# Queries and keys of one attention layer: computed with the channels on the partitions instead of the tokens

## The chip, the core and the metric

The kernel runs on one core of one Trainium2 chip. The metric is the device time of one execution in microseconds, as a median over runs. TensorE (PE) multiplies into PSUM banks of 512 f32 columns; VectorE (DVE), ScalarE (ACT) and GpSimd (POOL) work beside it, each through its own list of instructions in a fixed order; SyncE (SP) issues most of the DMAs, also in order.

## The reference

One layer: attention beside a state-space branch on the same normalised input, then an expert feed-forward part. The change touches only how `q` and `k` are made:

```python
q, k, v, z, xbc, dt_raw, gates = jnp.split(h @ w_in, IN_SPLITS, axis=-1)      # h: 1024 latent tokens x 1024
q = apply_rope(q.reshape(nb, ns, 8, 2, 64), cos, sin)
k = apply_rope(k.reshape(nb, ns, 8, 2, 64), cos, sin)
kc = (hc @ w_k).reshape(nb, nl, 8, 2, 64)                                     # hc: 256 context tokens, not rotated
k_all = jnp.concatenate([kc, k], axis=1)

def apply_rope(u, cos, sin):
    rot = jnp.concatenate([-u[..., 32:], u[..., :32]], axis=-1)
    return u * cos + rot * sin
```

A head has two components of 64 channels. The rotation mixes channel i of a component with channel i + 32, by the cosine and sine of the token's place.

## The kernel before

**Precision.** Every f32 operand is split into a high part (`hi`, `hh`) and a low rest (`lo`, `hl`), and each product is three matmuls (`mm3`, L419): high by high and two mixed ones.

**The stage.** `norm_and_qkv` (L491) normalises the ten token tiles of 128 (two of context, eight of latents), transposes them on PE (`modulate`, tiles `tr`), scales them (`hf`) and splits them into `hh` and `hl`, with the model channel on the partitions. The tokens are three groups g: 0 is the context (256 tokens), 1 and 2 are 512 latent tokens each. While the first inputs arrive, PE also makes the modulation vector (`ada`: tiles `wa`, `adab`). A second set of modulation products, `ada_late`, runs on DVE during the stage (tiles `wada`, `wacc`: eight instructions for each 512 KB loaded).

**The blocks.** `main` goes through six blocks of 512 output columns: k0, v0, q0, k1, v1, q1. Before the change each block goes token tile by token tile: for a tile, 24 matmuls with `hh` or `hl` (128 x 128, tokens) as the loaded operand and 512 weight columns streamed give tokens x 512 channels in one of four PSUM banks `acc`. In the first block the first three tiles are done by halves of the model channels, so that PE can begin with half of the weights.

**After a tile of q or k** comes `post_qk` (L661). A latent tile goes through three products on DVE (`ra`, and `rb` in two halves, with the table `rope`), a sum on POOL (`r`), four transposes on PE (f32, 128 x 128) into a bank `tr`, a copy by ACT to `sa` (the high part), a subtraction on DVE to `sb` (the low part), and, for every second tile, four or eight stores of `sa` and `sb` to the scratch tensor `qk` in DRAM. A context tile has a plain copy in the place of products and sum. `v` tiles are copied by ACT and stored.

**The order.** The kernel is written as generators; a scheduler (`Flow`, with estimated durations) interleaves them when the kernel is built, so what is written elsewhere may shift the order of instructions on every engine. The chip then follows that order. The mixer (`mixer_t`) begins when block q1 and all its `post_qk` are issued; its first piece is `dt` (16 + 16 matmuls of 512 columns and 16 of 256 with `hi`, folded by ten small matmuls `aux<-fold,G`, then a chain of DVE and ACT to the tile `dtn`), beside the first product of its convolution (`acc<-hh,hi` and so on).

Of the kernel before, what the change touches and what calls it, by code (L numbers as in the profile page):

```python
# [9 lines left out]
F32 = mybir.dt.float32  # L10
F32R = mybir.dt.float32r
# [3 lines left out]
ALU = mybir.AluOpType  # L15
# [4 lines left out]
P = 128  # L20
D = 1024
KC = 8
T = 1024
# [352 lines left out]
class Layer:  # L376
# [114 lines left out]
    def norm_and_qkv(s):  # L491


        nc, tc, I, F = s.nc, s.tc, s.I, s.F
# [7 lines left out]
        spans = [(0, 2), (2, 4), (6, 4)]  # L502
# [7 lines left out]
        acc = s.ring(pp, [P, 512], "acc", 4)  # L510
# [9 lines left out]
        st = {"wa": [], "x": 0, "w": 0, "normed": 0, "mod": 0, "done": [set(), set(), set()], "cols": 0, "blocks": 0, "ada": False, "q": None, "two": {}}  # L520
# [106 lines left out]
        def parts(g, k, hf, w):  # L627
# [5 lines left out]
            hfs.put(hf)  # L633
            st["done"][g].add(k)

        def weights():
            for n, (kind, j) in enumerate(blocks):
                c0 = {"q": COL_Q, "k": COL_K, "v": COL_V}[kind] + j * 512
                for a in (0, 4):
                    yield [raws, lambda: st["x"] >= (10 if n else AW0[a // 4]), "NOW"]  # L640
                    raw = raws.get()
                    F.dma(raw, win[:, a:a + 4, c0:c0 + 512])
                    st["w"] += 1
                    yield [lambda: sets[n % 2] is not None]
# [3 lines left out]
                    yield from s.splits([(hi[:, b:b + 2], lo[:, b:b + 2], raw[:, b:b + 2]) for b in (0, 2)],  # L648
                                        lambda raw=raw, w=(hi, lo): (raws.put(raw), ready.append(w)), 1)

        def post_v(ps, j, tok):
# [6 lines left out]
            F.dma(s.vv[j][tok], v[:, :512].rearrange("p (h d) -> p h d", d=P))  # L658
            sas.put(v)

        def post_qk(ps, kind, j, t):  # L661
            yield [lambda: st["q"] is not None]
            rr, ras, rbs, sas, sbs, rope = (st["q"][n] for n in ("r", "ra", "rb", "sa", "sb", "rope"))
            if t < 2:
                yield [ps, rr, "ACT"]
                r = rr.get()
                F.acopy(r, ps.rearrange("p (h x) -> p h x", x=64))
                acc.put(ps)
            else:
                yield [ps, rope, ras, rbs, "DVE"]  # L670
                cs = rope[:, t - 2, :]
                pv = ps.rearrange("p (h x) -> p h x", x=64)
                ra, rb = ras.get(), rbs.get()
# [3 lines left out]
                acc.put(ps)  # L677
                yield [ra, rb, rr, "POOL"]
                r = rr.get()
                F.ptt(r, ra, rb, ALU.add)  # L680
                ras.put(ra)
                rbs.put(rb)
            yield [r, tr]
            pt = tr.get()
            for m in range(4):
                F.tp(pt[:, m * P:(m + 1) * P], r[:, 2 * m:2 * m + 2].rearrange("p u x -> p (u x)"), s.ident)
            two = st["two"].setdefault((kind, j, t // 2), [])
            yield [pt, "ACT"] + ([] if two else [sas, sbs])
            if not two:
                two += [sas.get(), sbs.get(), 0]  # L690
            a, b = two[:2]
            (av, bv), pv = (w.rearrange("p (m h c) -> h p m c", m=4, h=2)[t % 2] for w in (a, b)), pt.rearrange("p (m c) -> p m c", m=4)
            F.acopy(av, pv)
            yield [a, "DVE"]
            F.tt(bv, pv, av.bitcast(F32), ALU.subtract)
            tr.put(pt)
            two[2] += 1
            if two[2] == 2:
                o0 = (t // 2 - (kind == "q")) * 2 * P
                dst = s.qk[j].rearrange("(m u) (v x) c -> v u x m c", u=2, v=2)  # L700
                for w, v, o in ((a, 0, 0), (a, 1, 0), (b, 0, T), (b, 1, T)) if kind == "q" else ((a, 0, 2 * T), (b, 1, 2 * T)):
                    for u in range(2):
                        F.dma(dst[v, u][:, :, o + o0:o + o0 + 2 * P], w[64 * u:64 * u + 64].bitcast(F32).rearrange("x (m c) -> x m c", m=4))
                sas.put(a)
                sbs.put(b)
            rr.put(r)

        def main():
            for n, (kind, j) in enumerate(blocks):
                tiles = list(range(2 if kind == "q" else 0, 10))  # L710
                steps = [(t, 0, KC) for t in tiles]
                if n == 0:
                    steps = [(t, a, a + 4) for a in (0, 4) for t in tiles[:NH]] + steps[NH:]
                banks = {}
                for t, k0, k1 in steps:
                    yield [lambda: len(ready) >= 2 * n + k1 // 4]
                    tok = slice(t * P, (t + 1) * P)
                    g = 0 if t < 2 else 1 if t < 6 else 2
                    sl = slice((t - spans[g][0]) * P, (t - spans[g][0] + 1) * P)
                    hh, hl = s.h[g]  # L720
                    yield [lambda: st["done"][g].issuperset(range(k0, k1))] + ([] if k0 else [acc])
                    ps = banks.pop(t) if k0 else acc.get()
                    for k in range(k0, k1):
                        wh, wl = ready[2 * n + k // 4]
                        if k % 4 == 0:
                            yield [wh, wl, hh, hl]
                        s.mm3(ps, hh[:, k, sl], hl[:, k, sl], wh[:, k % 4], wl[:, k % 4], k == 0, k == KC - 1)
                    if k1 < KC:
                        banks[t] = ps
                    else:  # L730
                        F.spawn(1, post_v(ps, j, tok) if kind == "v" else post_qk(ps, kind, j, t))
# [14 lines left out]
        F.run(lambda: st["ada"])  # L746
        s.close("wa")
        qp = s.open("qkv", side="right")
        st["q"] = q = {"r": s.ring(qp, [P, 8, 64], "r", 2), "ra": s.ring(qp, [P, 8, 64], "ra", 2),
                       "rb": s.ring(qp, [P, 8, 64], "rb", 2), "sa": s.ring(qp, [P, 1024], "sa", 2, F32R),  # L750
                       "sb": s.ring(qp, [P, 1024], "sb", 2, F32R), "rope": qp.tile([P, 8, P], F32, name="rope")}
        F.dma(q["rope"], I["rope"].rearrange("(t p) c -> p t c", p=P))
        F.run(lambda: len(st["done"][2]) == KC)
        s.close("xp")
        qw = s.open("qkvw1", side="right")
# [1728 lines left out]
```

## Time and profile before

| what | us |
|---|---|
| median of three runs (2785.47 to 2786.71) | 2785.7 |
| the profiled execution | 2800.41 |
| its span | 2798.6 |
| stage of the six blocks, first to last matmul | 31.5 to 386.9 |
| PE busy over the span | 94% |
| mean granted TensorE clock, share of full | 0.976 |

The profiled execution is 0.5% longer than the median. PE times overlap: a matmul of 512 columns is listed with about 0.39 us from start to modelled end, while the next starts about 0.23 us after it; what a matmul costs is read from start to start. The granted clock is 1.00 at 2.4 GHz and 0.5 at 1.2 GHz; a stretch between them has part of each.

### The profile page before, as it was taken

Reading aid. Unit: us, or ns where it says so; the run is one execution under the profiler, and the core shown is the slowest. Engines: PE = TensorE matmul, PEld = TensorE weight load, DVE = VectorE, ACT = ScalarE, POOL = GpSimd, SP = SyncE. Lnnn points to the kernel's source line nnn. Section 1 sums busy time; section 2 is a strip of 40 time slices with the busy share of each in tenths; the row PEclk is TensorE's granted clock in tenths of the full one; section 3 lists DMA queues with packets and bytes.
Section 4 is the critical chain, followed back from the end, with each engine's and each line's share of the span. In section 5 each row is a group of like instructions: output and inputs, shape, how many; then the busy total and the mean of one; then the engine's idle time right before and its main releaser. Section 6 shows DMA issues by size and latency. Waiting matters only on the chain.

```text
span 2798.6 us, 41131 instructions
## 1 busy us (share of the span) xinstructions
PE 2618.5 (94%) x14561; PEld 2101.1 (75%) x14561; DVE 2013.0 (72%) x4680; ACT 1340.7 (48%) x2104; POOL 903.0 (32%) x669
## 2 busy tenths in 40 slices
PE   7999999999999999999999999889999999999991
PEld 4888878778788777888887687668887776777660
DVE  6877133768686749888894767867788877788863
ACT  4211123344443546666664422435666656676651
POOL 0111010545353520000000000055656656677841
PEclk9999999999999999999999999999999999999996
DMA  7767253242334354223233953568899998999997
GB/s 277 224 206 216 64 143 105 67 139 91 121 91 132 106 172 145 82 91 141 93 102 125 292 179 133 188 216 264 276 309 297 315 299 278 307 321 328 314 316 233
DMA packets 275409, 545.67 MB, mean 195 GB/s; under 512 B 31562, under 2 KB 166835, under 8 KB 248194
## 3 DMA queue, kind: packets, MB, share of 16 engines
q1 hardware_dynamic: 239330, 437.14, 45.6%
q0 software_dynamic: 35872, 105.88, 14.8%
q8 instruction: 115, 1.88, 0.3%
q14 instruction: 92, 0.75, 0.1%
HBM read 433.78 MB, written 124.73 MB: 200 GB/s over the span
## 4 chain that ended last, share of the span: by engine, by line
PE 58%; DMA 10%; DVE 9%; issue 4%; ACT 2%; POOL 2%; SPq 0%; POOLq 0%; ACTq 0%; DVEq 0%
PE gu L148 16%; PE acc L148 10%; PE dn L148 9%; PE bacc L148 5%; PE sps L148 5%; PE pv L148 4%; DMA cr<-cumd,crow 3%; PE xt L152 2%; PE tr L152 2%; PE aux L148 2%; DVE G L187 2%; DMA qk<-qk 2%; DMA braw<-in_w_branch_attn_dram 1%; DVE gl L171 1%; DVE W L180 1%
## 5 line engine op out<-in xcount | busy, mean ns | idle before, releaser
L171 DVE TENSOR_TENSOR gl<-raw,gh 128x1024 fp32r<-128x1024 f32 x240 | 288.2, 1218 | 35.4 <-ACT gh L164 33.7
L148 PE MATMUL acc<-hh,hi 128*128 128x512 f32 (+2 forms) x760 | 304.7, 401 | 1.3 <-DVE ux L187 1.3
L148 PE MATMUL acc<-hl,hi 128*128 128x512 f32 (+2 forms) x760 | 289.3, 381 | 0.0
L164 ACT CAST gh<-raw 128x1024 fp32r<-128x1024 f32 x240 | 246.6, 1050 | 88.0 <-PE gu L148 59.2
L148 PE MATMUL acc<-hh,lo 128*128 128x512 f32 (+1 forms) x736 | 280.9, 382 | 2.5 <-DVE lo L171 2.5
L148 PE MATMUL gu<-gh,xh 128*128 128x512 f32 (+3 forms) x672 | 278.4, 414 | 0.6 <-ACT gh L164 0.6
L148 PE MATMUL gu<-gl,xh 128*128 128x512 f32 (+3 forms) x672 | 264.5, 394 | 6.2 <-DVE gl L171 4.4
L148 PE MATMUL gu<-gh,xl 128*128 128x512 f32 (+3 forms) x672 | 264.5, 394 | 0.0
L193 DVE TENSOR_SCALAR_CACHE_REDUCE e<-sps 128x512 f32<-128x512 f32 (+1 forms) x384 | 214.4, 597 | 32.9 <-PE sps L148 32.6
L262 POOL DMA_INDIRECT cr<-cumd,crow x98 | 123.4, 1260 | 316.1 <-DMA wtab<-sc 281.2
L268 POOL DMA_INDIRECT yacc<-y,tk x98 | 181.3, 1850 | 96.8 <-issue 23.2
L148 PE MATMUL sps<-qk 128*128 128x512 f32 (+1 forms) x768 | 195.6, 386 | 9.3 <-DMA qk<-qk 5.1
L156 ACT ACTIVATE e<-e,st 128x1280 f32<-128x1280 f32 x128 | 174.7, 1366 | 32.0 <-DVE st L202 31.8
L262 POOL DMA_INDIRECT wc<-wtab,tk x98 | 148.6, 1516 | 121.0 <-DVE tk L182 85.9
L148 PE MATMUL acc<-hi,hh 128*128 128x512 f32 x448 | 181.3, 405 | 0.0
L148 PE MATMUL acc<-hi,hl 128*128 128x512 f32 x448 | 176.2, 393 | 0.4 <-DVE hl L171 0.4
L148 PE MATMUL acc<-lo,hh 128*128 128x512 f32 x448 | 176.0, 393 | 0.0
L148 PEld LDWEIGHTS sps<-qk 128*128 128x128 f32 x768 | 141.2, 192 | 41.3 <-DVE e L193 8.3
L148 PEld LDWEIGHTS acc<-hh,hi 128*128 128x128 f32 (+1 forms) x760 | 142.6, 188 | 32.9 <-issue 4.0
L148 PE MATMUL pv<-wr,vv 128*128 128x256 f32 x640 | 165.1, 381 | 0.0
L148 PEld LDWEIGHTS acc<-hl,hi 128*128 128x128 f32 (+1 forms) x760 | 142.6, 188 | 27.4 <-issue 0.8
L148 PEld LDWEIGHTS acc<-hh,lo 128*128 128x128 f32 x736 | 138.7, 188 | 32.1 <-DVE lo L171 3.3
(327 smaller groups left out, 6264.3 us busy)
## 6 DMA issues: line engine op xcount, KB each, us to landing
raw<-in_w_e_gate_dram SPq DMA_DIRECT2D x64, 1024.0 KB
raw<-in_w_e_up_dram SPq DMA_DIRECT2D x64, 1024.0 KB
draw<-in_w_e_down_dram SPq DMA_DIRECT2D x64, 1024.0 KB
qk<-qk POOLq DMA_DIRECT2D x16, 1664.0 KB
raw<-in_w_in_dram SPq DMA_DIRECT2D x40, 512.0 KB
wada<-in_w_ada_dram SPq DMA_DIRECT2D x32, 512.0 KB
R<-acd SPq DMA_DIRECT2D x64, 256.0 KB
qk<-sa SPq DMA_DIRECT2D x52, 256.0 KB
```

The costliest lines, as they stand in the source:

```text
L148: s.nc.tensor.matmul(out, l, r, start=start, stop=stop)
L152: s.nc.tensor.transpose(out, in_, ident)
L156: s.nc.scalar.activation(out, in_, fn, **kw)
L164: s.nc.scalar.copy(out, in_)
L171: s.nc.vector.tensor_tensor(out, a, b, op=op)
L180: s.nc.vector.tensor_scalar(out, a, s1, s2, op0=op0)
L187: s.nc.vector.scalar_tensor_tensor(out, a, sc, b, op0=op0, op1=op1)
L193: s.nc.vector.tensor_scalar(out, a, s1, None, op0=op0, op1=op1, accum_out=acc)
L262: s.nc.gpsimd.indirect_dma_start(out=out, out_offset=None, in_=table, in_offset=bass.IndirectOffsetOnAxis(ap=idx, axis=0), **kw)
L268: s.nc.gpsimd.indirect_dma_start(out=table, out_offset=bass.IndirectOffsetOnAxis(ap=idx, axis=0), in_=in_, in_offset=None, compute_op=ALU. ...
```

## The change

For q and k the loaded and the streamed operand change places. A unit is now (token group g, half r of the eight components, rotary half f): its 24 matmuls load 128 weight columns and stream the group's 512 (or, for the context, 256) tokens, which gives channels x tokens. To have the 32 low channels of four components in one bank and the 32 high ones in another, the weights are reordered when they are split: `byhalf` writes them as (f, k, 256 channels), reading runs of 32. Two units, f = 0 and f = 1, make a pair of banks, and `post_qk` runs once for a pair: four products on DVE (two to `sb` in f32, two to `rb`), two sums on POOL, two copies by ACT to `sa`, two subtractions on DVE in place in `sb`, then the stores (128 partitions, 512 tokens each). The context pair has two copies and two subtractions straight from its banks. There is no transpose left in it, and the rings `r`, `ra` are gone. The table `rope` becomes 128 channels x (cos, sin) x 1024 tokens. Block k0 begins with units (1,0,0), (1,0,1), (0,0,0). `v` is as before.

```diff
-    rope = np.concatenate([cos, cos, -sin, sin], axis=-1).astype(np.float32)
+    rope = np.stack([np.tile(q.T, (4, 1)) for q in (cos, sin)], axis=1).astype(np.float32)
...
+        def byhalf(w):
+            return w.rearrange("p a b -> p (a b)").rearrange("p (f k c) -> p f k c", f=2, k=4)
...
+                    if kind != "v":
+                        parts = [[byhalf(w)[:, :, b:b + 2].rearrange("p f k (y i) -> p f (k y) i", i=32) for w in (hi, lo)] +
+                                 [raw[:, b:b + 2].rearrange("p k (y f i) -> p f (k y) i", f=2, i=32)] for b in (0, 2)]
...
-                F.tt(ra, pv, cs[:, None, 0:64].to_broadcast([P, 8, 64]), ALU.mult)
-                F.tt(rb[:, :, 0:32], pv[:, :, 32:64], cs[:, None, 64:96].to_broadcast([P, 8, 32]), ALU.mult)
-                F.tt(rb[:, :, 32:64], pv[:, :, 0:32], cs[:, None, 96:128].to_broadcast([P, 8, 32]), ALU.mult)
-                acc.put(ps)
-                yield [ra, rb, rr, "POOL"]
-                r = rr.get()
-                F.ptt(r, ra, rb, ALU.add)
...
-            for m in range(4):
-                F.tp(pt[:, m * P:(m + 1) * P], r[:, 2 * m:2 * m + 2].rearrange("p u x -> p (u x)"), s.ident)
...
-            F.acopy(av, pv)
-            yield [a, "DVE"]
-            F.tt(bv, pv, av.bitcast(F32), ALU.subtract)
...
+            yield [sbs, pair[0]]
+            lo = sbs.get(F32)
+            l = [lo[:, f * 512:f * 512 + n] for f in range(2)]
+            if g:
+                cos, sin = (rope[:, i, (g - 1) * 512:g * 512] for i in range(2))
+                yield [pair[0], rope, rbs, "DVE"]
+                rb = rbs.get()
+                F.tt(l[0], pair[0], cos, ALU.mult)
+                F.tt(rb[:, 1], pair[0], sin, ALU.mult)
+                acc.put(pair[0])
+                yield [pair[1], "DVE"]
+                F.tt(rb[:, 0], pair[1], sin, ALU.mult)
+                F.tt(l[1], pair[1], cos, ALU.mult)
+                acc.put(pair[1])
+                yield [rb, "POOL"]
+                F.ptt(l[0], l[0], rb[:, 0], ALU.subtract)
+                yield [rb, "POOL"]
+                F.ptt(l[1], l[1], rb[:, 1], ALU.add)
...
+            src = l if g else [b[:, :n] for b in pair]
...
+                F.acopy(hi[:, f * 512:f * 512 + n], src[f])
...
+                F.tt(l[f], src[f], hi[:, f * 512:f * 512 + n].bitcast(F32), ALU.subtract)
...
+                    units = [(g, r, f) for g in ((0, 1, 2) if kind == "k" else (1, 2)) for r in range(2) for f in range(2)]
+                    if n == 0:
+                        units = units[4:6] + units[:4] + units[6:]
...
-                        s.mm3(ps, hh[:, k, sl], hl[:, k, sl], wh[:, k % 4], wl[:, k % 4], k == 0, k == KC - 1)
...
+                            a, b = (byhalf(w)[:, u[2], k % 4, u[1] * P:(u[1] + 1) * P] for w in (wh, wl))
+                            s.mm3(ps[:, :spans[g][1] * P], a, b, hh[:, k], hl[:, k], k == 0, k == KC - 1)
```

The order of instructions moves at three places that matter below. In the lists a name is written `out<-inputs`, for matmuls `out<-streamed,loaded`; numbers tell tiles apart (`hh_81`, `hl_82` are group 0, `hh_83`, `hl_84` group 1, `hi_172`, `lo_173` the first half of the weights of k0, `x_87` on the token tiles).

PE at the start of the stage, before: the modulation products `acc<-wa,cw`, with the first block's matmuls on the context tiles among them.

```order
L152 MATMUL tr<-cst,x_88 128x128
L148 MATMUL acc<-wa,cw 32x512 x4
L148 MATMUL acc<-hi_172,hh_81 128x512
L148 MATMUL acc<-lo_173,hh_81 128x512
L148 MATMUL acc<-hi_172,hl_82 128x512
...
L148 MATMUL acc<-wa,cw 32x512 x4
...
L148 MATMUL adab<-fold,row 128x2 x4
L152 MATMUL tr<-cst,x_89 128x128
```

PE at the same place, now:

```order
L148 MATMUL acc<-wa,cw 32x512 x8
L148 MATMUL adab<-fold,row 128x2 x4
L152 MATMUL tr<-cst,x_89 128x128
...
L148 MATMUL adab<-fold,row 128x2 x4
L152 MATMUL tr<-cst,x_87 128x128
...
L148 MATMUL acc<-hh_83,hi_172 128x512
L148 MATMUL acc<-hl_84,hi_172 128x512
L148 MATMUL acc<-hh_83,lo_173 128x512
```

The 24 matmuls on context tiles that stood among the modulation products are gone from there; the first matmul of k0 is on group 1 and stands behind all of the modulation products and behind that group's transposes.

PE at the entry of the mixer, before: the folding of `dt`, then the first convolution product, with the small products on `dtn` among its matmuls.

```order
L148 MATMUL aux<-fold,G 128x32 x10
L148 MATMUL acc<-hh_83,hi 128x512
L148 MATMUL acc<-hl_84,hi 128x512
L148 MATMUL acc<-hh_83,lo 128x512
...
L148 MATMUL aux<-dtn,cst 128x160
L148 MATMUL acc<-hh_83,hi 128x512
```

PE at the same place, now:

```order
L148 MATMUL aux<-fold,G 128x32 x10
L148 MATMUL aux<-dtn,cst 128x160 x2
L148 MATMUL aux<-dtn,cst 128x320
L148 MATMUL aux<-cst,dtn 16x128 x4
L148 MATMUL acc<-hh_83,hi 128x512
```

The products on `dtn` now stand straight behind the folding, and nine convolution matmuls that stood between are behind them. From the next products on, the order of every engine is as before.

DVE in block q0, before: products, a group of eight `wacc`, the subtraction.

```order
L171 TENSOR_TENSOR ra<-acc,rope 128x512
L171 TENSOR_TENSOR rb<-acc,rope 128x8x32 x2
L180 TENSOR_SCALAR wacc<-wada,cc 128x128
L187 SCALAR_TENSOR_TENSOR wacc<-wada,cc,wacc 128x128 x7
L171 TENSOR_TENSOR sb<-tr,sa 128x4x128
```

DVE in block q0, now:

```order
L171 TENSOR_TENSOR sb<-acc,rope 128x512
L171 TENSOR_TENSOR rb<-acc,rope 128x512 x2
L171 TENSOR_TENSOR sb<-acc,rope 128x512
L180 TENSOR_SCALAR wacc<-wada,cc 128x128
L187 SCALAR_TENSOR_TENSOR wacc<-wada,cc,wacc 128x128 x7
L171 TENSOR_TENSOR sb<-sb,sa 128x512 x2
```

A pair's four products stand together behind its second unit, and its two subtractions behind one or two groups of `wacc`.

## Rows read from the trace of the kernel before

**Rows 1.** The page: span, and the chain that ended last, by engine.

```profile
span 2798.6 us, 41131 instructions
PE 58%; DMA 10%; DVE 9%; issue 4%; ACT 2%; POOL 2%; SPq 0%; POOLq 0%; ACTq 0%; DVEq 0%
```

**Rows 2.** Windows: length, busy us (count) of PE, PEld, DVE, ACT, POOL; clock; DMA.

```profile
47.00:61.00 14.00, 13.02 (x73) 10.34 (x73) 13.13 (x49) 8.90 (x17) 0.00 (x0) 1.00 0.48 158
140.00:210.00 70.00, 69.96 (x332) 57.55 (x331) 55.67 (x132) 10.89 (x16) 8.56 (x6) 1.00 0.67 206
280.00:350.00 70.00, 68.36 (x304) 55.95 (x302) 10.69 (x16) 10.37 (x18) 1.97 (x2) 1.00 0.22 65
```

**Rows 3.** Groups of instructions by line: the removed transposes, with the idle time before them.

```profile
L152 PE MATMUL tr<-cst,r 128*128 128x128 f32 x144 | 22.1, 276 | 6.8 <-POOL r L175 6.7
```

**Rows 4.** Timeline of PE around four transposes: start, duration, instruction.

```profile
377.83 0.39 PE L148 MATMUL acc<-hi,hl 128*128 128x512 f32 x1
378.06 0.60 PE L152 MATMUL tr<-cst,r 128*128 128x128 f32 x4
...
378.73 0.39 PE L148 MATMUL acc<-lo,hh 128*128 128x512 f32 x1
```

**Rows 5.** Timeline of PE at the end of block q1.

```profile
390.00 0.66 PE L152 MATMUL tr<-cst,r 128*128 128x128 f32 x4 [2.51 <-POOL r L175]
390.42 0.47 PE L148 MATMUL acc<-hh,hi 128*64 128x512 f32 x1
```

**Rows 6.** Windows behind it, columns as in rows 2.

```profile
392.00:395.00 3.00, 3.00 (x9) 1.61 (x8) 0.01 (x1) 0.81 (x2) 0.00 (x0) 0.58 0.80 185
405.00:409.00 4.00, 3.97 (x11) 2.77 (x12) 1.65 (x4) 3.95 (x6) 0.00 (x0) 0.60 0.52 127
```

**Rows 7.** Timeline of PE and DVE at the start of the stage.

```profile
31.53 0.79 PE L148 MATMUL acc<-hi,hh 128*128 128x512 f32 x1
47.39 0.48 PE L148 MATMUL acc<-hi,hh 128*128 128x512 f32 x1
60.88 0.69 DVE L171 TENSOR_TENSOR hl<-hf,hh 128x512 fp32r<-128x512 f32 x1
61.09 0.48 PE L148 MATMUL acc<-hi,hh 128*128 128x512 f32 x1
```

**Rows 8.** Timeline of PE in the mixer: matmuls of 256 columns.

```profile
422.35 0.28 PE L148 MATMUL acc<-hh,lo 128*128 128x256 f32 x1
422.47 0.28 PE L148 MATMUL acc<-hh,hi 128*128 128x256 f32 x1
```

**Rows 9.** Groups by line: the products and the subtraction of `post_qk`.

```profile
L171 DVE TENSOR_TENSOR sb<-tr,sa 128x512 fp32r<-128x512 f32 x36 | 24.5, 685 | 11.8 <-ACT sa L164 11.8
L171 DVE TENSOR_TENSOR rb<-acc,rope 128x256 f32<-128x256 f32 x64 | 23.9, 415 | 0.0
L171 DVE TENSOR_TENSOR ra<-acc,rope 128x512 f32<-128x512 f32 x32 | 22.0, 688 | 28.1 <-PE acc L148 26.3 <-PE adab L152 1.7
```

**Rows 10.** Timeline of PE at the entry of the mixer.

```profile
401.43 2.42 PE L148 MATMUL aux<-fold,G 64*128 64x32 f32 x20
403.78 0.50 PE L148 MATMUL acc<-hh,hi 128*128 128x512 f32 x1
...
408.33 0.54 PE L148 MATMUL aux<-dtn,cst 128*128 128x160 f32 x2
```

**Rows 11.** Timeline of SP: stores of q in block q0, a store of v.

```profile
158.47 0.33 SPq L212 DMA_DIRECT2D vv<-sa  x1
199.37 3.42 SPq L212 DMA_DIRECT2D qk<-sa  x4
```

**Rows 12.** Timeline of DVE and POOL in block q0.

```profile
182.66 1.29 POOL L175 TENSOR_TENSOR r<-ra,rb 128x512 f32<-128x512 f32 x1 [3.21 <-DVE rb L171]
182.72 3.71 DVE L187 SCALAR_TENSOR_TENSOR wacc<-wada,cc,wacc 128x128 f32<-128x128 f32 x7
187.25 2.67 DVE L187 SCALAR_TENSOR_TENSOR wacc<-wada,cc,wacc 128x128 f32<-128x128 f32 x7
```

More of the change, by code (lines that the diff above doesn't have):

```diff
@@ L659, in post_v, with post_qk @@
             sas.put(v)
-        def post_qk(ps, kind, j, t):
+        def post_qk(pair, kind, j, g, r):
             yield [lambda: st["q"] is not None]
-            rr, ras, rbs, sas, sbs, rope = (st["q"][n] for n in ("r", "ra", "rb", "sa", "sb", "rope"))
-            if t < 2:
-                yield [ps, rr, "ACT"]
-                r = rr.get()
-                F.acopy(r, ps.rearrange("p (h x) -> p h x", x=64))
-                acc.put(ps)
[L669 to L673, printed above, removed]
-                F.tt(ra, pv, cs[:, None, 0:64].to_broadcast([P, 8, 64]), ALU.mult)
-                F.tt(rb[:, :, 0:32], pv[:, :, 32:64], cs[:, None, 64:96].to_broadcast([P, 8, 32]), ALU.mult)
-                F.tt(rb[:, :, 32:64], pv[:, :, 0:32], cs[:, None, 96:128].to_broadcast([P, 8, 32]), ALU.mult)
-                acc.put(ps)
-                yield [ra, rb, rr, "POOL"]
-                r = rr.get()
-                F.ptt(r, ra, rb, ALU.add)
-                ras.put(ra)
-                rbs.put(rb)
-            yield [r, tr]
-            pt = tr.get()
-            for m in range(4):
-                F.tp(pt[:, m * P:(m + 1) * P], r[:, 2 * m:2 * m + 2].rearrange("p u x -> p (u x)"), s.ident)
[L687 to L692, printed above, removed]
-            F.acopy(av, pv)
-            yield [a, "DVE"]
-            F.tt(bv, pv, av.bitcast(F32), ALU.subtract)
[L696 to L706, printed above, removed]
@@ new lines, in post_qk @@
+            rbs, sas, sbs, rope = (st["q"][n] for n in ("rb", "sa", "sb", "rope"))
+            n = spans[g][1] * P
+            yield [sbs, pair[0]]
[16 more added lines that the diff above has]
+                F.ptt(l[1], l[1], rb[:, 1], ALU.add)
+                rbs.put(rb)
@@ new lines, in post_qk @@
+            src = l if g else [b[:, :n] for b in pair]
+            yield [sas]
+            hi = sas.get()
+            for f in range(2):
+                yield [src[f], "ACT"]
+                F.acopy(hi[:, f * 512:f * 512 + n], src[f])
+            for f in range(2):
+                yield [hi, "DVE"]
+                F.tt(l[f], src[f], hi[:, f * 512:f * 512 + n].bitcast(F32), ALU.subtract)
+            if g == 0:
+                acc.put(*pair)
+            o0 = (spans[g][0] - 2 * (kind == "q")) * P
@@ L708, in main @@
+            dst = s.qk[j].rearrange("(r y) (v f i) c -> r v f y i c", y=4, v=2, f=2)
+            for f in range(2):
+                for w, v, o in ((hi, 0, 0), (hi, 1, 0), (lo, 0, T), (lo, 1, T)) if kind == "q" else ((hi, 0, 2 * T), (lo, 1, 2 * T)):
+                    F.dma(dst[r, v, f][:, :, o + o0:o + o0 + n], (w[:, f * 512:f * 512 + n].bitcast(F32) if w is hi else l[f]))
+            sas.put(hi)
+            sbs.put(lo)
         def main():
             for n, (kind, j) in enumerate(blocks):
-                tiles = list(range(2 if kind == "q" else 0, 10))
@@ L711, in main @@
-                steps = [(t, 0, KC) for t in tiles]
+                if kind == "v":
+                    units = [(0 if t < 2 else 1 if t < 6 else 2, t) for t in range(10)]
+                else:
+                    units = [(g, r, f) for g in ((0, 1, 2) if kind == "k" else (1, 2)) for r in range(2) for f in range(2)]
+                    if n == 0:
+                        units = units[4:6] + units[:4] + units[6:]
+                steps = [(u, 0, KC) for u in units]
                 if n == 0:
-                    steps = [(t, a, a + 4) for a in (0, 4) for t in tiles[:NH]] + steps[NH:]
@@ L714, in main @@
-                banks = {}
-                for t, k0, k1 in steps:
+                    steps = [(u, a, a + 4) for a in (0, 4) for u in units[:NH]] + steps[NH:]
+                banks, done = {}, {}
+                for u, k0, k1 in steps:
+                    g = u[0]
                     yield [lambda: len(ready) >= 2 * n + k1 // 4]
-                    tok = slice(t * P, (t + 1) * P)
-                    g = 0 if t < 2 else 1 if t < 6 else 2
-                    sl = slice((t - spans[g][0]) * P, (t - spans[g][0] + 1) * P)
@@ L720, in main @@
                     hh, hl = s.h[g]
                     yield [lambda: st["done"][g].issuperset(range(k0, k1))] + ([] if k0 else [acc])
-                    ps = banks.pop(t) if k0 else acc.get()
+                    ps = banks.pop(u) if k0 else acc.get()
                     for k in range(k0, k1):
@@ L726, in main @@
                             yield [wh, wl, hh, hl]
-                        s.mm3(ps, hh[:, k, sl], hl[:, k, sl], wh[:, k % 4], wl[:, k % 4], k == 0, k == KC - 1)
+                        if kind == "v":
+                            sl = slice((u[1] - spans[g][0]) * P, (u[1] - spans[g][0] + 1) * P)
+                            s.mm3(ps, hh[:, k, sl], hl[:, k, sl], wh[:, k % 4], wl[:, k % 4], k == 0, k == KC - 1)
+                        else:
+                            a, b = (byhalf(w)[:, u[2], k % 4, u[1] * P:(u[1] + 1) * P] for w in (wh, wl))
+                            s.mm3(ps[:, :spans[g][1] * P], a, b, hh[:, k], hl[:, k], k == 0, k == KC - 1)
                     if k1 < KC:
-                        banks[t] = ps
-                    else:
-                        F.spawn(1, post_v(ps, j, tok) if kind == "v" else post_qk(ps, kind, j, t))
+                        banks[u] = ps
+                    elif kind == "v":
+                        F.spawn(1, post_v(ps, j, slice(u[1] * P, (u[1] + 1) * P)))
+                    else:
+                        two = done.setdefault(u[:2], [])
+                        two.append(ps)
+                        if len(two) == 2:
+                            F.spawn(1, post_qk(two, kind, j, *u[:2]))
                 ws = ready[2 * n:2 * n + 2]
@@ L748, in norm_and_qkv @@
         qp = s.open("qkv", side="right")
[L749 to L752, printed above, removed]
+        st["q"] = q = {"rb": s.ring(qp, [P, 2, 512], "rb", 2),
+                       "sa": s.ring(qp, [P, 1024], "sa", 2, F32R),
+                       "sb": s.ring(qp, [P, 1024], "sb", 2, F32R), "rope": qp.tile([P, 2, T], F32, name="rope")}
+        F.dma(q["rope"], I["rope"])
         F.run(lambda: len(st["done"][2]) == KC)
```

5 lines of the change are left out of this document (3 added, 2 removed).

## The prediction

> **What bounds the kernel now.** I read the page first: PE is the largest part of the chain that ended last [rows 1], and the stage of the change lies 390 us into a span of 2798.6. Then the windows: in 140 to 210 us PE is busy for 69.96 of 70 us and DVE for 55.67; in 280 to 350, where only v is computed, PE is busy for 68.36 and nothing else is full [rows 2]. So from about 61 us on the stage is bound by PE. What a matmul costs there is 70 us / 304 = 0.230 us for 512 columns [rows 2]. Only the start is different: between 47 and 61 us DVE is busy for 13.13 of 14 us [rows 2], making the groups' `hh` and `hl`. Last I read the timelines at the two ends of the stage, where PE waits. Behind the entry of the mixer the order of every engine is unchanged, so I pass on to the end of the kernel, one for one, what PE has gained or lost when the first convolution product is done.
>
> **Transposes, removed.** There are 144 in groups of four [rows 3]. A group costs what it delays: the last matmul before it starts at 377.83, the second one behind it at 378.73 [rows 4]; two steps of 0.23 would be 0.46, so the group costs 0.90 - 0.46 = 0.44 us. 36 groups make **-15.8 us**, on PE, which is the bound. PE was also idle in front of them, 6.7 us for the sum of POOL [rows 3], of which 2.51 at the very end [rows 5]. No PE instruction waits for POOL now: **-6.7 us** (at least -2.5, if other waits take the place of those in the middle).
>
> **Clock at the end, given back.** Behind the idle 2.51 us the granted clock was 0.58 in 392 to 395 us [rows 6]. Those 3 us had 0.42 of 2.4 GHz missing, so they cost 3 x 0.42 = **-1.3 us**; now `dt` follows the last matmul of q1 directly, since its first bank was emptied two pairs earlier.
>
> **Matmuls, the same columns.** q and k have 384 matmuls each of 512 columns for the latents, as before; the context has 192 of 256 columns in place of 96 of 512. In the mixer matmuls of 256 columns start 0.12 us apart with a full 128 x 128 load [rows 8], so 192 x 0.12 = 23.0 against 96 x 0.23 = 22.1: under 1 us, taken as **0**. Bounds 0 and +2.
>
> **The start, lost.** Before, PE began k0 at 31.53 us, between the modulation products, and went on at 47.39 [rows 7]. By 61.09, when `hl` of group 1 was complete (its last piece at 60.88) [rows 7], it had done 60 matmuls, nearly all on the context. Now the three units that come first hold 24 matmuls on group 1 and 12 of half length, worth 30. They can't start before about 47 us, since the first four channel chunks of group 1 were ready only then, and the second halves wait for its last four chunks at about 61, since these hang on ACT and DVE, not on PE. So PE is idle there for some us, and 60 - 30 = 30 matmuls come later: 30 x 0.23 = **+6.9 us**. An idle PE there also falls back to the low clock, one spell like that of rows 6: **+1.3**. Bounds +4.6 (20 matmuls, no spell) and +12 (half of the first units at 1.2 GHz too, with the modulation products slower before them).
>
> **The entry of the mixer, lost.** Before, nine convolution matmuls covered the chain from the folding to `dtn`: PE went on at 403.78 and the first product on `dtn` came at 408.33 [rows 10]. Now this product stands directly behind the folding, so 408.33 - 403.78 = 4.5 us are idle. Three small products in a row add about 1.0 for the copies between them. The folding, which took 2.42 us because it waited for copies [rows 10], gets these earlier (the last pair's products end some 3 us after the last matmul) and shrinks by about 1.3. The low clock follows as it did before, when 405 to 409 us had 0.60 [rows 6]. Sum **+4.2 us**; bounds 0 (all of it hidden by a wait that I don't see now) and +8.
>
> **DVE, ACT, POOL, SP: off the path, taken as 0.** For two latent tiles DVE had two `ra`, four `rb` and two `sb` [rows 9], by listed durations 2 x 0.69 + 4 x 0.415 + 2 x 0.685 = 4.4 us; now a pair has six instructions of 512 elements, 6 x 0.69 = 4.1. POOL has 32 sums as before and ACT 40 copies of equal total size. Reading in runs of 32 elements costs DVE nothing where rows have it: `rb` did so. For ACT no row has such runs; if its casts of q and k weights took twice as long they would still be a block ahead. What hides DVE's lag is PSUM: a pair's banks must be free 11 us after its second unit (two units of 24 x 0.23 = 5.5), where a tile's bank had 16.5 before. Bounds 0 and +6. The stores are as many for q and k in bytes, with rows of 2 KB in place of 1 KB: four took SP 3.42 us, while a store of v, 128 rows of 2 KB, took 0.33 [rows 11]. So SP gets shorter.
>
> One row speaks against the new subtraction. A group of seven `wacc` took 2.67 us alone, and 3.71 when a sum on POOL of 1.29 us lay beside it [rows 12], about 1.0 us more. The Trainium skill (SBUF — State Buffer, section "SBUF: two separate sides") says why: VectorE with two SBUF inputs and a GpSimd instruction that reads SBUF exclude each other for a whole instruction. By that rule the 32 latent subtractions, which had one input in PSUM before and now have both in SBUF, could be held up too; the trace agrees for `wacc`, and no run here shows it for the subtraction. It is the push behind the first rival.
>
> **The sum.** -15.8 - 6.7 - 1.3 + 6.9 + 1.3 + 4.2 = **-11.4 us** on the profiled execution's 2800.41 us, that is 2789.0, a factor of 0.9959. The median of the runs was 2785.7, 0.5% under the profiled one; times 0.9959 it is **2774 us**. With the bounds the same case reaches from about -19 to -3: 2767 to 2783.
>
> **The rivals.**
> - *Nothing gained (2784).* The two ends eat it: the start costs 12 and the entry 8, and half of the waits for POOL come back as waits for a bank: -15.8 - 4.6 - 1.3 + 12 + 8 = -1.7. For it: DVE had 80% of 140 to 210 us [rows 2], and a pair's products come all at once. Against it: the 36 groups are certain, and the start's loss is capped by what PE did early, 60 matmuls or 13.8 us.
> - *Slower (2800).* One mechanism: the two `sb` buffers. A pair takes one at its first product and gives it back when the last of its four stores has landed, so DVE can't start pair i + 2 before pair i's has landed, and everything behind on DVE waits, then PE for its banks. The place is q0 and k1, eight latent pairs with `wacc` between products and subtraction. Price: with a holding time H, a pair takes H / 2 instead of 11; the first 11 us of delay are free. It decides from H = 22. From rows, products, two groups of `wacc` (2 x 3.7 [rows 12]), subtractions and four stores on SP are 2.8 + 7.4 + 1.3 + 3.4 = 15 us, so landing may take 7. At H = 31 it is 8 x (15.5 - 11) - 11 = +25, less the 11 gained: 2785.7 + 14 = 2800. Against it: before, the buffers were held likewise and no PE wait for a bank shows, and SP's part gets shorter.
> - *More (2764).* Start and entry cost only their lower bounds and nothing else comes up: -15.8 - 6.7 - 1.3 + 4.6 + 0 = -19, and one or two more if DVE, a little lighter, brings group 2 earlier.
>
> **How the numbers follow.** The forecast has 0.66, nothing gained 0.17, slower 0.10, more 0.07. About 0.2% (5.6 us) is what a measurement of this kernel can tell from no change. Of the forecast's case 0.63 lies under 2780.1 and 0.03 above; with "more" that is 0.70 faster; 0.19 within 0.2%; and slower than 2791.3 are 0.10 and a remainder of nothing gained, 0.11. For 8 in 10 the range takes the forecast's whole case, the greater part of nothing gained and a piece of "more": **2766 to 2786**.
>
> **What would show it.** The trace after should have no transposes of `r`; 512-column matmuls at 0.23 us in k and q, as in v; an idle PE of some us between about 55 and 62 us; the last matmul of q1 at about 377 us, 10 us earlier; PE idle for 4 to 6 us behind `aux<-fold,G`; and the same distance as before from the first convolution product to the end. I am wrong if PE waits for DVE in front of `acc` in q0 or k1, if DVE waits for DMA in front of `sb<-acc,rope`, if the first unit of k0 comes much later than 47 us, or if matmuls with weights loaded and tokens streamed run at another pace than the reverse.

## The result and the profile after

The changed kernel takes 2863.1 us (median of five runs, 2861.8 to 2864.2); its ratio to the kernel before is 1.0279, 95% interval 1.0265 to 1.0293, so it is some 77 us slower where 2774 had been forecast. What is asked of the profile is where these 77 us stand, and with them the 11 that should have been won.

The page of after, span and chain, beside [rows 1]: PE went from 58% to 63% of the chain of a longer span, and DMA from 10% to 16%.

```profile
span 2862.4 us, 41012 instructions
PE 63%; DMA 16%; DVE 10%; issue 4%; POOL 2%; ACT 2%; SPq 1%; POOLq 0%; DVEq 0%; ACTq 0%
```

Windows of after (columns as in [rows 2]): in blocks q0 and k1 PE now stands still for some 36% and 25% of the time, at a granted clock of 0.78 to 0.83. In the last window, q1 and `dt`, the 16 DMA engines are busy for 0.27 of the time.

```profile
210.00:280.00 70.00, 44.80 (x219) 39.40 (x218) 30.92 (x69) 8.24 (x12) 8.52 (x6) 0.78 0.40 138
280.00:350.00 70.00, 52.26 (x209) 41.46 (x208) 34.22 (x81) 7.79 (x12) 7.59 (x6) 0.83 0.41 139
430.00:480.00 50.00, 31.75 (x148) 23.87 (x147) 10.79 (x17) 9.49 (x15) 5.06 (x4) 0.81 0.27 103
```

Waits of after in 30 to 480 us (engine, line, waited for: sum, times, longest). The last three, 69 us of PE, have no counterpart in the kernel before, where PE's longest sum is 6.7 us, for POOL [rows 3].

```profile
DVE sb L171 <- DMA qk<-sb: 64.9, 7, 19.8
DVE wacc L180 <- DMA wada<-in_w_ada_dram: 60.3, 17, 11.2
PE adab L148 <- DVE wacc L187: 38.4, 7, 9.5
PE acc L148 <- DVE sb L171: 20.1, 4, 13.8
PE acc L148 <- DVE rb L171: 10.9, 2, 9.7
```

PE waits for DVE, and DVE for DMAs: for its `sb` buffers, which the stores to `qk` still read, and for the loads of `wada`. So the stores were looked at next. The timeline of SP in block q1 of after:

```profile
417.72 2.99 SPq L212 DMA_DIRECT2D qk<-sa  x4
420.76 10.34 SPq L212 DMA_DIRECT2D qk<-sb  x4
431.21 9.77 SPq L212 DMA_DIRECT2D qk<-sa  x4
441.08 10.51 SPq L212 DMA_DIRECT2D qk<-sb  x4
451.69 9.81 SPq L212 DMA_DIRECT2D qk<-sa  x4
```

Only the first four go out in 3 us. From there on four stores of 256 KB need 10 us, eight of them (one pair of q, 2 MB) about 20.6, which is 102 GB/s; before, eight took 3.2 + 3.9 us. Share of the 16 DMA engines in 40 slices of 1.25 us (tenths), in block q1 of the kernel before:

```profile
DMA  0000896390000899989600199988930059998970
```

and in block q1 of after:

```profile
DMA  3222222222222222222222222222222222223222
```

Before, a burst of stores keeps nearly all engines busy and is over; after, the share stays at a quarter without a pause. That this is four engines at full pace, and not sixteen at a quarter of it, can be counted from the DMA packets in the traces: in 435 to 465 us of after exactly four are in flight for 85% of the time, and a packet of 2 KB takes 84 ns. What differs is the shape: a store wrote 64 x 4 x 256 elements to DRAM, and writes 4 x 32 x 512 now, since the four components of a bank lie far apart in the scratch tensor. Both have 256 KB.

Down the chain it looks so. DVE, at the start of a pair in q1:

```profile
442.05 0.69 DVE L171 TENSOR_TENSOR sb<-acc,rope 128x512 f32<-128x512 f32 x1 [11.73 <-DMA qk<-sb]
```

and PE, whose `dt` needs a bank that DVE has not emptied:

```profile
447.82 0.40 PE L148 MATMUL acc<-hh,hi 128*64 128x512 f32 x1
465.46 0.69 PE L148 MATMUL acc<-hh,hi 128*64 128x512 f32 x1 [13.77 <-DVE sb L171]
```

The first matmul of `dt` comes at 447.8 us where it was at 390.4 [rows 5].

### The profile page after: what moved, and what is told of

It is laid out like the page before. It is cut to its first block, busy times and chain, and to the rows that moved or that the text cites. A ratio compares the mean times of both kernels' runs of the same rounds, so it can differ in the third digit from the quotient of the medians.

```text
span 2862.4 us, 41012 instructions
## 1 busy us (share of the span) xinstructions
PE 2618.2 (91%) x14513; PEld 2101.5 (73%) x14513; DVE 2002.6 (70%) x4652; ACT 1340.2 (47%) x2104; POOL 902.5 (32%) x669
## 4 chain that ended last, share of the span: by engine, by line
PE 63%; DMA 16%; DVE 10%; issue 4%; POOL 2%; ACT 2%; SPq 1%; POOLq 0%; DVEq 0%; ACTq 0%
PE acc L148 15%; PE gu L148 15%; PE dn L148 9%; PE bacc L148 5%; PE sps L148 5%; PE pv L148 4%; DMA cr<-cumd,crow 3%; DMA wada<-in_w_ada_dram 3%; PE tr L152 2%; PE xt L152 2%; DMA qk<-sb 2%; PE aux L148 2%; DVE G L187 2%; SPq L212 1%; DMA qk<-qk 1%
## 5 line engine op out<-in xcount | busy, mean ns | idle before, releaser
L148 PE MATMUL acc<-hh,hi 128*128 128x512 f32 (+3 forms) x1080 | 432.0, 400 | 33.2 <-DVE sb L171 20.1
L148 PE MATMUL acc<-hl,hi 128*128 128x512 f32 (+3 forms) x1080 | 413.2, 383 | 0.0
L148 PE MATMUL acc<-hh,lo 128*128 128x512 f32 (+1 forms) x1056 | 404.8, 383 | 2.3 <-DVE lo L171 2.3
L148 PEld LDWEIGHTS acc<-hh,hi 128*128 128x128 f32 (+1 forms) x1080 | 207.8, 192 | 77.3 <-DVE sb L171 20.9
L148 PEld LDWEIGHTS acc<-hl,hi 128*128 128x128 f32 (+1 forms) x1080 | 207.9, 192 | 38.0 <-issue 0.6
L148 PEld LDWEIGHTS acc<-hh,lo 128*128 128x128 f32 x1056 | 203.5, 193 | 43.2 <-DVE lo L171 2.8
L175 POOL TENSOR_TENSOR sb<-sb,rb 128x512 f32<-128x512 f32 x32 | 42.7, 1354 | 424.3 <-DVE rb L171 386.6
L148 PEld LDWEIGHTS sps<-qk 128*128 128x128 f32 x768 | 139.3, 189 | 42.8 <-DVE e L193 10.3
L262 POOL DMA_INDIRECT xg<-htab,tk x98 | 131.7, 1344 | 81.9 <-PE hT L152 32.2
L148 PEld LDWEIGHTS gu<-gh,xh 128*128 128x128 f32 (+3 forms) x672 | 122.1, 182 | 36.9 <-issue 8.3
```

The lines of the kernel that those rows point to most:

```text
L148: s.nc.tensor.matmul(out, l, r, start=start, stop=stop)
L175: s.nc.gpsimd.tensor_tensor(out, a, b, op=op)
L262: s.nc.gpsimd.indirect_dma_start(out=out, out_offset=None, in_=table, in_offset=bass.IndirectOffsetOnAxis(ap=idx, axis=0), **kw)
```

## The experiments

Three theories. **H1**: the store's outer dimension of 4 keeps it on 4 of the 16 engines. **H2**: two `sb` buffers are too few, whatever the stores. **H3**: the loads of `wada` are late because they are queued behind the stores in SP's list. Ratios are to runs of the kernel before on the same chip. The kernel before took 2784 us beside experiments 1, 2, 3 and 7 and 2798 beside the others, so between these groups only ratios are compared.

**1. The scratch tensor in another order.** The rows that a store writes now lie one behind the other; the read gathers them.

```diff
-            dst = s.qk[j].rearrange("(r y) (v f i) c -> r v f y i c", y=4, v=2, f=2)
+            dst = s.qk[j].rearrange("(r v f) p c -> r v f p c", v=2, f=2)
...
-                    F.swdma(t, s.qk[h // 4][2 * (h % 4) + c])
+                    u = 2 * (h % 4) + c
+                    F.swdma(t, s.qk[h // 4].rearrange("(r w) (y i) c -> r y i w c", w=4, y=4)[u // 4, u % 4])
```

> After, with only the scratch tensor of q and k laid out otherwise: the four components' rows of one rotary half stand one behind the other, so that a store of 128 partitions goes to one list of 128 equally spaced rows in place of 4 lists of 32. The same stores in number, bytes, row length and order; the read of a component gathers its rows as 32 x 4. H1 (the outer dimension of 4 keeps a store on a quarter of the DMA engines, 0.26 busy and about 102 GB/s in block q1 of the trace after): eight stores of a pair take SP 3 to 6 us in place of 20.6, the DMA share in q1 goes over 0.6 in bursts, DVE waits no longer for stores in front of sb<-acc,rope, and the kernel takes 2774 us (2767 to 2783), the sum of the prediction. H2 (too few sb buffers, whatever the store's form): nothing of that, 2850 or more. H3 (the stores' place ahead of the wada loads in SP's list): 2850 or more as well, since the list is the same.

Measured: 2765.9 us, ratio 0.9940 (0.9928 to 0.9952), a little under what H1 expected. The order of the rows in DRAM alone is worth 97 us (94 by the ratios). SP in block q1 of this kernel:

```profile
353.26 2.08 SPq L212 DMA_DIRECT2D qk<-sa  x4
355.44 3.00 SPq L212 DMA_DIRECT2D qk<-sb  x4
364.46 2.07 SPq L212 DMA_DIRECT2D qk<-sa  x4
```

A pair takes SP some 5 us in place of 20.6, and in 353 to 358 us sixteen or more packets are in flight for 93% of the time. A packet of 2 KB takes 86 ns, as good as the 84 of after, so it isn't the writing of single rows that was slow. H2 and H3 had forecast no change here.

**2. Outer dimension 2.**

```diff
-                    F.dma(dst[r, v, f][:, :, o + o0:o + o0 + n], (w[:, f * 512:f * 512 + n].bitcast(F32) if w is hi else l[f]))
+                    wv = w[:, f * 512:f * 512 + n].bitcast(F32) if w is hi else l[f]
+                    for y in (0, 2):
+                        F.dma(dst[r, v, f][y:y + 2, :, o + o0:o + o0 + n], wv[32 * y:32 * y + 64])
```

> After, with each store of q and k cut in two, 2 x 32 rows each: the same bytes, twice the stores, outer dimension 2. H1: two engines carry them, about 51 GB/s, a pair of q takes SP some 41 us in place of 20.6; eight pairs of q and four of k later that is 8 x 20 + 4 x 10 = 200 us more at most, 2990 to 3070. H2 and H3: the bytes and the buffers are the same, SP has twice the instructions to issue; 2863 to 2880.

Measured: 3122.1 us, ratio 1.1214 (1.1195 to 1.1233). SP in block q1:

```profile
589.83 13.82 SPq L212 DMA_DIRECT2D qk<-sa  x8
603.75 20.37 SPq L212 DMA_DIRECT2D qk<-sb  x8
```

and the window around these stores (columns as in [rows 2]):

```profile
590.00:650.00 60.00, 33.63 (x145) 25.91 (x143) 10.28 (x14) 3.11 (x5) 5.42 (x5) 0.80 0.13 49
```

Half a store takes the same 2.55 us as a whole one did: the rate is halved, as H1 has it, and so is the share, 0.13. By the packets of 610 to 640 us two are in flight for 90% of the time, at 84 ns each, and the rows in DRAM are those of after. The kernel lost 260 us more than after, over the upper bound of 200. The sum counted four pairs of k where there are eight latent ones (k0 and k1); with eight it gives 8 x 20 + 8 x 10 = 240. Where the rest falls wasn't separated.

**3. The loads of `wada` on ACT's queue.**

```diff
-                F.dma(w, wada[:, :, c0:c0 + P])
+                F.dma(w, wada[:, :, c0:c0 + P], s.nc.scalar)
```

> After, with the 32 loads of wada issued by ACT and no longer behind the stores in SP's list; the stores stay as they are. H1 with the stores' own pace as the limit: four engines still take 20.6 us for a pair of q, DVE waits for its sb buffer as before, and each wada load still has a quarter of its rows behind the stores on those engines; 2850 to 2870, the waits of PE for wacc (38 us in the stage) turn into waits for sb. H3 (the loads are late because they are queued behind the stores on SP): the wada waits go and with them 30 to 38 us, 2825 to 2835.

Measured: 2860.5 us, ratio 1.0281 (1.0260 to 1.0302), no change. Its waits show why:

```profile
PE acc L148 <- DVE sb L171: 32.2, 4, 13.4
PE adab L148 <- DVE wacc L187: 19.7, 6, 4.7
PE acc L148 <- DVE rb L171: 14.7, 2, 8.7
```

Most of what PE waits less for `wacc` (38.4 to 19.7) it waits more for `sb` (20.1 to 32.2) and `rb` (10.9 to 14.7). For the loads of `wada` H3 falls as a cause; SP's list is one of the ways on which the rate reaches PE. Issuing the stores themselves elsewhere wasn't tried.

**4. A third `sb` buffer** (and one `rb`, for room).

```diff
-        st["q"] = q = {"rb": s.ring(qp, [P, 2, 512], "rb", 2),
+        st["q"] = q = {"rb": s.ring(qp, [P, 2, 512], "rb", 1),
...
-                       "sb": s.ring(qp, [P, 1024], "sb", 2, F32R), "rope": qp.tile([P, 2, T], F32, name="rope")}
+                       "sb": s.ring(qp, [P, 1024], "sb", 3, F32R), "rope": qp.tile([P, 2, T], F32, name="rope")}
```

> After, with three sb buffers in place of two (and one rb in place of two, to make room); the order of instructions is the same on every engine, the stores too. H1, by rate: a pair of q still needs 20.6 us of the four engines against 11 us of matmuls, so a third buffer only moves the delay by one pair in each of the blocks: 2840 to 2865. H2, by holding time (the price of the prediction's slower rival, H / 2 per pair, with three buffers H / 3 = 41 / 3 = 14 us): three quarters of the loss go, 2785 to 2805.

Measured: ratio 1.0275 (1.0253 to 1.0297); after has 1.0279. In the stage PE hardly waits for `sb` any more, and more for `wacc` (38.4 in after):

```profile
PE adab L148 <- DVE wacc L187: 53.3, 8, 11.9
PE acc L148 <- DVE sb L171: 4.8, 1, 4.8
```

Behind the stage, where after waited 13.77 us for `sb` among its `dt` products, PE now goes on, and waits in the mixer instead:

```profile
PE acc L148 <- DVE ux L187: 16.8, 1, 16.8
DVE G L198 <- DMA acd<-G: 32.2, 1, 32.2
```

`acd<-G` is a store of the mixer. SP issues it behind the last stores of q1, at 494.13 us, and in after at 495.79: SP is done with the stores at nearly the same time (491.6 and 493.2 us), whatever the buffers. A buffer more moves the wait and leaves the time: it is a rate, not a holding time. H2 falls, with the reserve that one `rb` buffer went for the third `sb`; PE's wait for `rb` (10.9 in after) is gone all the same.

**5. Half of the bytes on sixteen engines.** The second copy of each bank is stored by component, 32 rows each.

```diff
+                    wv = w[:, f * 512:f * 512 + n].bitcast(F32) if w is hi else l[f]
+                    if v == 0:
+                        F.dma(dst[r, v, f][:, :, o + o0:o + o0 + n], wv)
+                    for y in range(4 * v):
+                        F.dma(dst[r, v, f][y, :, o + o0:o + o0 + n], wv[32 * y:32 * y + 32])
```

> After, with the stores of the second copy (half of all bytes) cut into four of 32 rows each, which have 32 as their outer dimension, while the first copy keeps its 4 x 32. H1: a pair of q has 1 MB on four engines (10.3 us at 102 GB/s) and 1 MB on sixteen (about 3 to 4 us), 13 to 14 us in place of 20.6, against 11 us of matmuls; of the 97 us between after (2863) and merged rows (2766) a quarter or less is left, 2770 to 2795. H2 and H3: SP has 20 stores for a pair in place of 8, in the same place, with the same bytes; 2850 to 2880.

Measured: ratio 1.0181 (1.0159 to 1.0203), about 2834 us if the kernel before is put at 2784: faster than after, but far from 2795. SP in block q1 (two stores of 256 KB and eight of 64 KB in a row):

```profile
386.37 8.61 SPq L212 DMA_DIRECT2D qk<-sa  x10
395.08 8.79 SPq L212 DMA_DIRECT2D qk<-sb  x10
403.98 8.80 SPq L212 DMA_DIRECT2D qk<-sa  x10
```

A pair takes 17.6 us, not 13 to 14. Whether SP's issue sets this or the engines that are still busy with the large ones wasn't separated: the large stores take SP some 0.52 us each here and not 2.55, and the share of the DMA engines in 395 to 440 us is 0.55. This run has the rows in DRAM of after, and half of its bytes in other stores; that alone wins back 0.010 of the 0.034 between the ratios of after and of experiment 1. The loss still goes with SP's time for a pair: (17.6 - 11) / (20.6 - 11) of 97 us is 67, and 2766 + 67 = 2833. The planner's order moves in some places too, so this is a sum that fits rather than a proof.

**6. The kernel before, with outer dimension 4, and its twin with 16.** Everything on PE, DVE and ACT is as before, transposes included; only the rows of the scratch tensor lie otherwise (a = 4 or 16).

```diff
-                dst = s.qk[j].rearrange("(m u) (v x) c -> v u x m c", u=2, v=2)
+                dst = s.qk[j].rearrange("p q c -> (p q) c").rearrange("(a v u b m) c -> v u a (b m) c", a=4, v=2, u=2, m=4)
```

> The kernel before, with the rows of the scratch tensor of q and k in another order, the same for both: the 64 channels of a component lie as 4 x 16, and the 16 together with the four pairs of components are 64 rows one behind the other, so that a store has 4 as its outer dimension. The order of instructions on PE, DVE and ACT, the number of stores, their bytes and their rows of 1 KB are those of before, the transposes too. H1: the same 2.55 us of four engines for a store of 256 KB as in after, eight of them 20.4 us against 11.9 us of PE for two tiles; after lost 97 us by an excess of 9.6, so this loses some 86: 2850 to 2890, more (up to 3000) if rows of 1 KB go slower there than rows of 2 KB. H2 and H3 and whatever else lies in the new compute of after: 2780 to 2795.

> Its twin: the kernel before with the 64 channels laid as 16 x 4, so that the outer dimension of a store is 16 and 16 rows lie together; everything else as in its twin, also the read that gathers rows. H1: sixteen engines as before, 2775 to 2790. If gathering rows, and not the outer dimension, costs the time, it is as slow as its twin.

Measured: with 4, ratio 1.0480 (1.0448 to 1.0511); with 16, 0.9998 (0.9983 to 1.0013). SP in block q1, with 4:

```profile
450.04 10.77 SPq L212 DMA_DIRECT2D qk<-sa  x4
460.92 10.74 SPq L212 DMA_DIRECT2D qk<-sb  x4
```

and with 16:

```profile
366.41 2.90 SPq L212 DMA_DIRECT2D qk<-sa  x4
369.41 3.98 SPq L212 DMA_DIRECT2D qk<-sb  x4
```

So the old computation becomes as slow as the new one, and slower, by the order of the rows alone, and the twin's gather costs nothing. The loss is 134 us where 86 were expected. By the traces the first matmul of `dt` comes 77 us later than before (467.2 against 390.4). PE then waits once for 20.3 us in the mixer, for DVE, which waits for `acd<-G`; SP issues it behind the last stores of q1, as in experiment 4. And attention, which reads these rows, takes 460 us from its first to its last score where it had 426. In that stage of the kernel with 4:

```profile
PE sps L148 <- DMA qk<-qk: 29.2, 7, 6.8
```

This wait was 5.1 us before. Why its read became slower, when its twin's did not, wasn't tried and stays open; the comparison of the stores rests on the stage ahead of `dt`.

**7. The start: context first again** (with merged rows).

```diff
-                    if n == 0:
-                        units = units[4:6] + units[:4] + units[6:]
```

> The kernel with merged rows, and block k0 in its plain order again, context pairs first, so that PE has context matmuls among the modulation products. The prediction's term for the start (30 matmuls later and a spell of low clock, +8.2 us): this kernel is 5 to 9 us faster than the one with merged rows alone, 2766 if that takes 2774. Rival: the start is bound by the products of DVE and ACT for group 1 and by the loads, not by PE's count of matmuls, and the early context matmuls only put off the transposes: within 3 us of the one with merged rows.

Measured: 2763.3 us, ratio 0.9928 (0.9913 to 0.9942) against 0.9940 with merged rows alone; the intervals overlap. By the traces `dt` begins at 370.27 in place of 372.73 us: 2.5 us, half of the lower bound. That is within the 3 us of the rival.

**8. The entry of the mixer filled** (with merged rows and the context first).

```diff
-                    yield [dtn, aux]
+                    yield [F.ready[_n(dtn)] + 4000.0, aux]
```

> The kernel with merged rows and the context first, and the first product on dtn held back in the planner by 4 us, so that nine convolution matmuls stand between the folding and it, as in the kernel before. The prediction's term for the entry of the mixer (4.2 us; 3.6 us from the first dt matmul to the third convolution product by the trace of the merged rows): PE waits no longer 4.5 us for dtn, and the kernel takes 3 to 4 us less than the one with the context first, 2760 in place of 2763. Rival: the convolution matmuls wait for the low part of their weights in that place and the chain behind dtn comes later by as much; within 1.5 us of 2763.

Measured: ratio 0.9916 (0.9899 to 0.9933), against 0.9928: not told apart from no change. The nine convolution matmuls stand in the gap again, but their weights aren't there:

```profile
385.71 0.79 PE L148 MATMUL acc<-hh,hi 128*128 128x512 f32 x1 [3.93 <-ACT hi L164]
```

From the first `dt` matmul to the third convolution product it takes 37.5 us in place of 38.0. By the trace the rival was right; by the ratios, 3 us apart with intervals of 4 to 5 us to either side, the two can't be told apart. This is the fastest of all kernels by its ratio, though not surely faster than the two before it.

## Why the prediction was wrong, step by step

**The step that failed** is the last sentence on the stores: "with rows of 2 KB in place of 1 KB: four took SP 3.42 us, while a store of v, 128 rows of 2 KB, took 0.33 [rows 11]. So SP gets shorter." It took the length of a row and the number of bytes for the whole shape, and left out that the outer dimension in DRAM falls from 64 to 4. For a store that is 128 rows indeed the reading was right: with merged rows four take SP 2.07. The term was put at 0 without bounds of its own; it measured 97 us. Experiments 1, 2 and 6 show it from both sides: SP needs 20.6 us for a pair with 4, 40.7 with 2, about 5 with 128 rows; and 21.5 with 4 against 7 with 16 in the old computation. The packets in flight, four in after, two in experiment 2 and sixteen in experiment 1, say the same.

The Trainium skill (DMA: Bandwidth & Descriptors, section "Why a DMA increments its semaphore by 16 and not by 1") states it: a DMA is spread over the largest number of engines up to 16 that divides the slowest dimension, other than 1, of both of its sides. By that a store of 4 x 32 x 512 has 4 engines although its SBUF side has 128 partitions. The trace agrees: a share of 0.27, and half the rate with 2. The page also says which engines these are, the lowest-numbered ones; no run here shows that. The rule that the prediction weighed against the change was a smaller one.

**How the rate becomes time.** A pair of q has 48 matmuls of 0.233 us, 11.2 us, and needs 20.6 us of stores, 9.4 too many; a latent pair of k has half the bytes (10.3 us). Where PE falls behind can be read from the first matmuls of q0, v1 and `dt`, in after:

```profile
188.39 0.48 PE L148 MATMUL acc<-hh,hi 128*128 128x512 f32 x1
348.53 0.47 PE L148 MATMUL acc<-hi,hh 128*128 128x512 f32 x1
447.82 0.40 PE L148 MATMUL acc<-hh,hi 128*64 128x512 f32 x1
```

and with merged rows (`dt` at 372.73, below):

```profile
169.58 0.48 PE L148 MATMUL acc<-hh,hi 128*128 128x512 f32 x1
273.43 0.47 PE L148 MATMUL acc<-hi,hh 128*128 128x512 f32 x1
```

- Up to q0: 18.8 us. PE waits for `wacc` there, 12.6 us, that is for loads of `wada` beside the stores of k0.
- q0 and k1: 160.1 us in place of 103.9, 56 more. The four pairs of q at 9.4 us make 38 of it; the rest, `wada` loads and the pairs of k among them, wasn't separated.
- v1 and the matmuls of q1: 99.3 us in both kernels. The pairs of q1 hold up nothing yet.
- From the first `dt` matmul to the third convolution product: 54.3 us in place of 39.3, 15 more. This is what q1 costs.

Together that is 90 of the 97 us. The other 7 come later and weren't followed. Eight pairs of q at 9.4 us would make 75 us too, the delay of `dt`, but by chance: all of that delay is there before q1 begins. The sum of experiment 6 (eight times the excess) rests on the same count.

**The slower rival** (2800) named the right place, q0 and k1, and one of the chains, `sb` held until its stores have landed, DVE waiting, PE without a bank; the other, the late loads of `wada`, it didn't have. Two things of it were wrong. It took four stores at SP's 3.4 us of before, so that 7 us were left for the landing; in after four stores take SP 10 us. And its price, H / 2, takes the buffers for the limit: with a third buffer nothing was won, since four engines were busy all the time. A holding time can be bought off with buffers, a rate can't.

**The other terms** can be read in the kernel with merged rows, which is the change without the mistake, at the first `dt` matmul. PE in its stage:

```profile
46.66 0.48 PE L148 MATMUL acc<-hh,hi 128*128 128x512 f32 x1
59.19 0.48 PE L148 MATMUL acc<-hh,hi 128*128 128x512 f32 x1
372.73 0.40 PE L148 MATMUL acc<-hh,hi 128*64 128x512 f32 x1
412.03 0.40 PE L148 MATMUL acc<-hh,hi 128*128 128x512 f32 x1
```

- *Transposes and waits for POOL* (-15.8, -6.7): the stage ends 390.42 - 372.73 = 17.7 us earlier. With the start taken out (next point) that is -22.8 against -22.5. Right as a sum; the two weren't measured apart.
- *The start* (+6.9 and +1.3): the second halves began at 59.19, not 61, and by 61.1 PE had done 24 + 6 + 8 = 38 matmuls where it had done 60 [rows 7]: 22 x 0.23 = +5.1. No spell of low clock: 47 to 61 us had 1.00. Too dear by 3.1, and experiment 7 could win back only 2.5.
- *Clock at the end and entry* (-1.3 + 4.2 = +2.9): from the first `dt` matmul to the third convolution product it takes 412.03 - 372.73 = 39.3 us, and took 35.7 before: +3.6. PE waits 4.47 us for `dtn`, the 4.5 of the prediction. Right, though experiment 8 shows that the nine matmuls that covered it before don't fill it now: their weights come too late.
- *256 columns* (0): they start 0.12 us apart. Right.
- *DVE and ACT* (0): the windows with merged rows show PE full.

```profile
61.00:140.00 79.00, 79.00 (x408) 67.06 (x406) 66.61 (x133) 21.65 (x32) 10.33 (x8) 1.00 0.63 203
140.00:210.00 70.00, 70.00 (x321) 57.79 (x320) 54.98 (x127) 11.15 (x16) 7.59 (x6) 1.00 0.70 226
210.00:280.00 70.00, 70.00 (x361) 59.26 (x360) 56.89 (x117) 15.10 (x22) 14.67 (x10) 1.00 0.63 200
```

The subtraction with both inputs in SBUF has a mean of 765 ns where [rows 9] had 685, so 2.6 us of DVE in all, and nothing of it reaches PE. The mean hides two kinds (min/median/max in ns):

```profile
L171 DVE TENSOR_TENSOR sb<-sb,sa x32: 678/685/1115, 72.0 to 376.9; 128x512 f32<-128x512 f32 x32
```

Of the 32, 26 took about 685 ns as before, and six 1108 to 1115. These six, and no others, began while a sum on POOL was running (for some 0.56 us more): the exclusion that the prediction weighed is there, six times.

Sum at the entry: -17.7 + 3.6 = -14.1, forecast -11.4. The runs give -13 to -20 us for that kernel. Attention is 5.7 us shorter there by the traces (420.3 in place of 426.0 us from first to last score; PE waits 1.0 us for the read of `qk`, not 5.1); its read gathers rows in another order, and that this is the cause is only argued. So the arithmetic on PE, which took most of the prediction's room, was good to 3 us, and one term left at 0 was worth 97.

## What to carry to other kernels

When a layout changes, write down every DMA's dimensions on both sides, as issued, before its bytes: the outermost one on the DRAM side (2, 4 or 16 and more), not the row length or the number of partitions, went here with how many engines worked. In a profile a DMA share that stays flat at a simple fraction (0.27 here) while one queue's issues grow long is the sign, and another order of rows in the scratch tensor was the cure here. Before paying for buffers or other queues, compare the bytes of one step, at the measured rate, with the time of the step.

## What the runs showed of the hardware

- Stores of 256 KB as 4 x 32 x 512: 2.55 us each in a row, 102 GB/s; as 2 x 32 x 512 half the bytes in the same 2.55; as 128 x 512 or 16 x 16 x 256 SP went on after 0.5 to 1.0 us. At 4, rows of 1 KB (21.5 us for eight) were nearly as fast as rows of 2 KB (20.6).
- The packets in flight were four, two and sixteen for outer dimensions of 4, 2 and 128, and one of 2 KB took 84 to 86 ns in each: fewer engines worked, none was slower.
- SP shows nothing of it at first: the first four stores went out in 2.99 us, and only the next were slow. A short issue time is no proof of a fast DMA.
- Of 32 subtractions on DVE with both inputs in SBUF the six that began beside a running sum on POOL took 1.11 us, the others 0.685.
